# Fetching the next octet's gates and activations in quarters, spread over the weights of v, instead of whole

## The chip, the cores and the metric

The kernel runs on one core of a Trainium2 chip, in one launch. The metric is device time in microseconds (us). Three runs of the kernel before gave 2525.65, 2525.91 and 2526.83 us; their median, 2525.91, is the time before. A separate profiled execution took 2525.12 us. Engines: TensorE (PE), VectorE (DVE), ScalarE (ACT), GpSimd (POOL) and SyncE (SP), which here only issues DMAs.

## The reference, cut to what matters

The program is two transformer blocks on 512 tokens of width 1024. The first block and most of the second (attention, convolutions, gated mixing) lie ahead of the place of the change. The change lies in the last part, a layer with 16,384 experts of which every token uses 128:

```python
def chunk(args):
    hx, idx, g = args
    a = jax.nn.gelu(jnp.einsum("ced,cd->ce", u_emb[idx], hx), approximate=False)
    return jnp.einsum("ce,ced->cd", g * a, v_emb[idx])
...
x = x + peer(h2, w_peer_q[l], peer_sub_keys[l], peer_u[l], peer_v[l])
return rmsnorm_2(x, final_g)
```

For each token, 128 rows of the table `u_emb` are multiplied with the token, a gelu follows, and 128 rows of the table `v_emb` are summed with the weights `g * a`.

## The kernel before, in words

The 512 tokens are treated in two ways. For the last 384 tokens (`TD`) the kernel computes with all experts, as dense matrix products: the activations gelu(u·h) of all 16,384 experts, times a dense gate that is zero for unused experts, times v. For the first 128 tokens it gathers the used rows: 128 rows of u and then 128 rows of v per token. One gather brings one 128x1024 float32 tile (one row of the table per token, 512 KB) by an indirect DMA that POOL issues; DVE then consumes it with one instruction. There are 256 such row tiles in all (128 of u, 128 of v).

The dense part has two phases. In the u phase, 128 products of u are made in 16 groups of eight, called octets. Each octet's activations (a 128 x 8 x 384 tile, 1536 KB) go out to DRAM (`a_dr`), but for the last two octets, which stay (`NRES` = 2). The gates, made by one-hot products beside it, go to DRAM too (`g_dr`, 1536 KB per octet).

The v phase, in which the change lies, runs over 128 units (16 octets of 8) in the order `VORD`: the two octets that stayed, then the other 14. One unit is one 128x1024 slice of v (512 KB) and 24 matmuls of 384 columns on PE (`mix`, for 8 output tiles three products each of split high and low parts). For each unit:

- `weighted` (L1317) makes activation times gate on DVE (`wv`), its high part on ACT and its low part on DVE (`wv..l`). It runs `WAHEAD` = 2 units ahead of PE. It reads the gate tile `goct` (two buffers, one octet each) and the activation tile `acts` (two buffers, shown as `last` in the profile).
- `feed` (L255) loads v in pairs of units (1024 KB, tile `raw`, two buffers) on SP's DMA queue, and splits each unit: the high part on ACT (`w..h`), the low part on DVE (`w..l`). A pair is loaded as soon as both of its buffer's units are split. In unit `i` the program splits unit `i + 2`.
- `row_step` (L1054) consumes one or two gathered row tiles on DVE (`yt <- row, ea, yt` or `yt <- last, ea, yt`), so that all are done shortly before the end (`quota`). There are four row buffers (`NROW`): tiles named `row`, and the spare ends of the `last` tiles. POOL issues the gather into a buffer when DVE has consumed it.

Every engine works its instructions in the order in which the program was written, and so does each DMA queue: SP's queue carries the loads of v, of the gates and of the activations, in that order of issue; POOL's queue carries the gathers. What sets the order around the change is the main loop (L1355): at the first unit of an octet it issues `fetch_g` (the whole gate tile of the next octet) and `fetch_a` (its whole activation tile), both on SP's queue, then the rest of the unit. PE's `acc <- wv50l, w358h` is unit 50: the weights of unit n are named w(308+n), so unit 48, the first of octet 6, has wv48 and w356.

Of the kernel before, what the change touches and what calls it, by code (L numbers as in the profile page):

```python
# [10 lines left out]
F32 = mybir.dt.float32  # L11
# [10 lines left out]
P = 128  # L22
# [7 lines left out]
NOCT = 16  # L30
# [10 lines left out]
TC = 16  # L41
TD = T - P
NTC = TD // TC
WAHEAD = 2
NRES = 2
VORD = list(range(NOCT - 1, NOCT - 1 - NRES, -1)) + list(range(NOCT - NRES))
# [143 lines left out]
def body(tc, a):  # L190
    nc = tc.nc
# [4 lines left out]
    with ExitStack() as ctx:  # L196
        ctx.enter_context(tc.manual_schedule())

        def mkpool(stack, name, **k):
            return stack.enter_context(tc.tile_pool(name=name, bufs=1, **k))  # L200
# [90 lines left out]
        def unit(ahead=AHEAD):  # L291
            i = st["use"]
            feed(i + 1 + ahead)
            st["use"] += 1
            return parts.pop(i)
# [22 lines left out]
        wk = mkpool(ph, "wk")  # L318
# [440 lines left out]
        for g in range(2):  # L759
            c = 64 * g  # L760
# [248 lines left out]
        wk = mkpool(ph, "wk2")  # L1009
# [44 lines left out]
        def row_step():  # L1054


            n = rows[0]
            rows[0] += 1
            fetch_row(n + NROW)
            r, e = row_buf(n), ea[:, n % P:n % P + 1]  # L1060
            if n < P:
                V.tensor_tensor_reduce(r, r, h2t[0], 1.0, 0.0, ALU.mult, ALU.add, e)
            elif n == P:
                V.tensor_scalar(yts[0], r, e, None, ALU.mult)
            else:
                V.scalar_tensor_tensor(yts[0], r, e, yts[0], ALU.mult, ALU.add)
            if n == P - 1:
                S.activation(ea, ea, AF.Gelu)
                V.tensor_tensor(ea, ea, eg, ALU.mult)
# [114 lines left out]
        g_dr = dr.tile([NOCT, P, NTC, 8, TC], F32, name="g_dr")  # L1184
        a_dr = [dr.tile([P, 8, TD], F32, name=f"a_dr{o}") for o in range(NOCT - NRES)]
# [57 lines left out]
        aocts = {}  # L1243
        acts = []
# [42 lines left out]
        octs = {}  # L1287
        yts = []

        def last_phase():  # L1290

            nonlocal wk, ph, NT2
            ph.close()
            ph = ExitStack()
            ctx.enter_context(ph)
            wk = mkpool(ph, "wk3")
            NT2 = 12
            yts.append(wk.tile([P, D], F32, name="yt"))
            h2t.append(wk.tile([P, D], F32, name="h2s"))
            S.activation(h2t[1], h2tok, AF.Copy)  # L1300
            del h2t[0]
            fetch_g(0)

        def fetch_g(n):
            if n < NOCT:
                go = wk.tile([P, NTC, 8, TC], F32, tag="goct", name=f"goct{n}", bufs=2)
                nc.sync.dma_start(go, g_dr[VORD[n]])
                octs[n] = go

        def fetch_a(n):  # L1310
            if n < NOCT and VORD[n] not in aocts:
                aocts[VORD[n]] = acts[(n + 1) % 2]
                nc.sync.dma_start(aocts[VORD[n]], a_dr[VORD[n]])

        ready = {}

        def weighted(i):  # L1317

            n, j = divmod(i, 8)
            ao, go = aocts[VORD[n]], octs[n]  # L1320
            w, h, l = t2(f"wv{i}"), t2(f"wv{i}h", F32R), t2(f"wv{i}l", F32R)
            d = slice(P, T)
            V.tensor_tensor(w[:, d].rearrange("p (c t) -> p c t", c=NTC),
                            ao[:, j].rearrange("p (c t) -> p c t", c=NTC), go[:, :, j, :], ALU.mult)
            S.activation(h[:, d], w[:, d], AF.Copy)
            yield
            V.tensor_tensor(l[:, d], w[:, d], h[:, d].bitcast(F32), ALU.subtract)
            if i == 0:
                S.activation(l[:, :P], ident, AF.Copy, scale=0.0)
            if j == 7:  # L1330
                del octs[n]
            ready[i] = h, l
# [9 lines left out]
        def mix(m, q, first, last):  # L1342

            wh, wl, vh, vl = q
            c = slice(m * P, (m + 1) * P)
            d = slice(P, T)
            e = slice(0, T) if first else d
            PE.matmul(acc8[m][:, e], vh[:, c], wl[:, e], start=first, stop=False)
            PE.matmul(acc8[m][:, d], vl[:, c], wh[:, d], start=False, stop=False)
            PE.matmul(acc8[m][:, d], vh[:, c], wh[:, d], start=False, stop=last)  # L1350
# [2 lines left out]
        row0, yt = rows[0], yts[0]  # L1353
        NV = 8 * NOCT
        for i in range(NV - NLAST):  # L1355
            if i % 8 == 0:
                fetch_g(i // 8 + 1)
                fetch_a(i // 8 + 1)

            quota = min(2 * P, row0 + 4 + i * (2 * P - row0) // (NV - 12))  # L1360
            w = weighted(i + WAHEAD)
            next(w)
            if rows[0] < quota:
                row_step()
            list(w)
            while rows[0] < quota:
                row_step()
            q = ready.pop(i) + unit()
            for m in range(KT):
                mix(m, q, i == 0, False)  # L1370
# [152 lines left out]
```

## Time and profile before

| | before |
|---|---|
| median of 3 runs | 2525.91 us |
| profiled execution, its own time | 2525.12 us |
| its span, first to last instruction | 2523.4 us |
| PE busy over the span | 2404.9 us (95%) |
| DVE busy over the span | 1774.1 us (70%) |
| v phase, first product to the last octet's start | 1865.6 to 2470.5 us |

Times of the trace are counted from the first instruction. The v phase is the last quarter of the span. An octet's start is read off PE's timeline as the first product with that octet's first `wv`. In the views, "idle before" is the time for which an engine stood still ahead of an instruction, with what it waited for; "DMA share" is the mean busy share of 16 DMA engines (it can pass 1.00 by a little, as packets overlap at their ends), and "PEclk" is TensorE's granted clock as a share of its full speed. A matmul's shown duration includes its passage through the engine; the pace is read from start to start.

### The profile page before, as it was taken

To read this page: it belongs to the slowest core of one execution; us is meant where nothing else is said; L and a number is where in the kernel's file an instruction comes from. 1 tells how busy PE (TensorE), PEld (TensorE's weight loads), DVE (VectorE), ACT (ScalarE), POOL (GpSimd) and SP (SyncE) were. 2 spreads that over 40 slices of the span, in tenths; PEclk is the share of its full clock that TensorE was granted. 3 is DMA by queue.
4 is the path that set the end of the run, shared out by engine and by line. 5 is a ranking of instruction groups with operands and counts; after the bars stand their busy time and mean duration, and the time that the engine had idled before them with its cause. 6 is when DMAs were issued, how large, how long until landed. Compare 5 with 4: busy or idle time off the path is not lost.

```text
span 2523.4 us, 33808 instructions
## 1 busy us (share of the span) xinstructions
PE 2404.9 (95%) x13113; PEld 2135.8 (85%) x13121; DVE 1774.1 (70%) x3172; ACT 1022.2 (41%) x1558; POOL 747.6 (30%) x581
## 2 busy tenths in 40 slices
PE   9999999999999999999999999999998988898987
PEld 7777888888776668888899999999998988898887
DVE  4647644433468888556799999975577878787885
ACT  4454423322355665533233457653332323232333
POOL 2122011100137767003252300022234434444431
PEclk9999999999999999999999999999999999899998
DMA  4110222222211112222245568888889998999982
GB/s 164 57 51 34 105 100 85 99 101 100 84 51 51 51 51 100 85 99 92 91 155 189 184 219 266 270 303 300 305 305 373 331 368 334 371 337 361 358 322 90
DMA packets 128896, 466.13 MB, mean 185 GB/s; under 512 B 9184, under 2 KB 60512, under 8 KB 95200
## 3 DMA queue, kind: packets, MB, share of 16 engines
q1 hardware_dynamic: 39456, 281.04, 30.4%
q0 software_dynamic: 36864, 134.23, 14.7%
q10 hardware_dynamic: 52416, 48.70, 5.8%
q8 instruction: 103, 1.69, 0.3%
q14 instruction: 57, 0.47, 0.1%
HBM read 414.65 MB, written 49.28 MB: 184 GB/s over the span
## 4 chain that ended last, share of the span: by engine, by line
PE 44%; issue 25%; DVE 11%; DMA 10%; POOL 7%; ACT 3%; POOLq 0%; DVEq 0%; SPq 0%; ACTq 0%
PE u L133 8%; PE up L133 5%; DMA last<-in_vn,eid 5%; PE gate L133 5%; DMA row<-in_vn,eid 4%; PE pq L133 3%; POOL last L1045 3%; POOL row L1045 3%; PE acc L133 2%; PE wo L133 2%; DVE yt L133 2%; PE qkb L133 2%; PE ao L133 2%; PE gc L133 2%; PE co L133 2%
## 5 line engine op out<-in xcount | busy, mean ns | idle before, releaser
L133 POOL TENSOR_TENSOR cy<-cy,cvt 128x511 f32<-128x511 f32 (+14 forms) x120 | 170.7, 1422 | 59.2 <-ACT cvt L133 42.9
L1045 POOL DMA_INDIRECT last<-in_un,eid x64 | 74.0, 1156 | 342.2 <-DVE ea L133 317.4
L133 ACT ACTIVATE last<-u 128x384 f32<-128x384 f32 x128 | 63.4, 495 | 251.8 <-PE u L133 251.6
L1045 POOL DMA_INDIRECT last<-in_vn,eid x64 | 88.8, 1388 | 103.4 <-DVE yt L133 95.3
L1045 POOL DMA_INDIRECT row<-in_vn,eid x64 | 87.1, 1360 | 106.5 <-DVE yt L133 96.1
L1045 POOL DMA_INDIRECT row<-in_un,eid x64 | 75.7, 1183 | 123.4 <-DVE ea L133 120.7
L133 ACT ACTIVATE stage<-gp 128x512 f32<-128x512 f32 x96 | 95.9, 1106 | 36.7 <-PE gp L133 20.4
L133 DVE SCALAR_TENSOR_TENSOR yt<-row,ea,yt 128x1024 f32<-128x1024 f32 x64 | 82.1, 1283 | 37.1 <-DMA row<-in_vn,eid 37.1
L133 DVE SCALAR_TENSOR_TENSOR yt<-last,ea,yt 128x1024 f32<-128x1024 f32 x63 | 80.8, 1283 | 38.1 <-DMA last<-in_vn,eid 38.0
L133 DVE TENSOR_TENSOR hot<-hot,ijb 128x1024 bf16<-128x1024 bf16 x144 | 91.4, 687 | 1.6
L133 DVE SCALAR_TENSOR_TENSOR cyp<-u,par,cyp 128x511 f32<-128x511 f32 (+28 forms) x116 | 85.4, 736 | 2.4
L133 ACT ACTIVATE cvt<-u,par 128x511 f32<-128x511 f32 (+14 forms) x120 | 78.6, 701 | 0.7 <-DVE u L133 0.7
L133 PEld LDWEIGHTS <-hot 128*128 128x128 bf16 x1152 | 66.4, 97 | 13.1 <-DVE hot L133 8.5
L133 PE MATMUL gp<-hot,hot 128*128 128x128 bf16 x1152 | 74.7, 219 | 2.7 <-DVE hot L133 2.6
L133 DVE TENSOR_TENSOR wv<-last,goct 128x384 f32<-128x384 f32 x128 | 70.9, 554 | 0.0
L133 DVE TENSOR_TENSOR hot<-iota,ijb 128x1024 bf16<-128x1024 bf16 x96 | 61.8, 686 | 0.1
L133 DVE CUSTOM_DVE_ANT_0 last<-last,h2s 128x1024 f32<-128x1024 f32 x34 | 41.6, 1223 | 23.8 <-DMA last<-in_un,eid 23.8
L133 DVE CUSTOM_DVE_ANT_0 row<-row,h2s 128x1024 f32<-128x1024 f32 x36 | 44.0, 1223 | 12.5 <-DMA row<-in_un,eid 12.5
L133 DVE TENSOR_TENSOR su<-up,n2r 128x512 f32<-128x512 f32 x22 | 15.2, 691 | 51.7 <-PE up L133 51.7
L133 DVE MAX8 stop__8676<-skc 128x8 f32<-128x128 f32 x128 | 36.8, 287 | 5.5 <-ACT skc L133 3.2
L133 PEld LDWEIGHTS o<-v,pT 128*128 128x128 f32 x224 | 27.8, 191 | 14.8 <-ACT pT L133 7.6
L133 DVE CUSTOM_DVE_ANT_0 last<-last,h2tok 128x1024 f32<-128x1024 f32 x30 | 36.5, 1216 | 5.1 <-DMA last<-in_un,eid 5.1
(6461 smaller groups left out, 8606.2 us busy)
## 6 DMA issues: line engine op xcount, KB each, us to landing
raw<-in_w SPq DMA_DIRECT2D x89, 1024.0 KB, 4.8
raw<-in_u SPq DMA_DIRECT2D x64, 1024.0 KB, 6.4
raw<-in_v SPq DMA_DIRECT2D x64, 1024.0 KB, 7.7
g_dr<-stage ACTq DMA_DIRECT2D x24, 1024.0 KB, 7.0
goct<-g_dr SPq DMA_DIRECT2D x16, 1536.0 KB, 12.5
a_dr<-last ACTq DMA_DIRECT2D x14, 1536.0 KB, 10.0
last<-a_dr SPq DMA_DIRECT2D x14, 1536.0 KB, 17.3
xT<-in_x_t SPq DMA_DIRECT2D x1, 1024.0 KB, 9.5
```

Source lines behind the costliest of these rows:

```text
L133: return f(*args, **kw)
L1045: nc.gpsimd.indirect_dma_start(row_buf(n), None, t, bass.IndirectOffsetOnAxis(ap=eid[:, n % P:n % P + 1], axis=0))
```

## The change

The gate tile and the activation tile of the next octet are each fetched by four DMAs in place of one. The gates' quarters are cut by token (six of 24 groups of 16 tokens each), the activations' by product (two of eight). The gates' quarters are issued at units 0, 1, 2 and 3 of the running octet, the activations' at units 2, 3, 4 and 5. For octets that stayed (`n < NRES`) no activations are fetched, as before. The first gate tile is fetched in four DMAs as well, all at once.

```diff
-        def fetch_g(n):
-            if n < NOCT:
-                go = wk.tile([P, NTC, 8, TC], F32, tag="goct", name=f"goct{n}", bufs=2)
-                nc.sync.dma_start(go, g_dr[VORD[n]])
-                octs[n] = go
-
-        def fetch_a(n):
-            if n < NOCT and VORD[n] not in aocts:
-                aocts[VORD[n]] = acts[(n + 1) % 2]
-                nc.sync.dma_start(aocts[VORD[n]], a_dr[VORD[n]])
+        def fetch_g(n, quarters=range(4)):
+            for q in quarters if n < NOCT else ():
+                if q == 0:
+                    octs[n] = wk.tile([P, NTC, 8, TC], F32, tag="goct", name=f"goct{n}", bufs=2)
+                c = slice(q * NTC // 4, (q + 1) * NTC // 4)
+                nc.sync.dma_start(octs[n][:, c], g_dr[VORD[n]][:, c])
+
+        def fetch_a(n, q):
+            o = VORD[min(n, NOCT - 1)]
+            if n < NOCT and (q > 0 or o not in aocts) and n >= NRES:
+                aocts[o] = acts[(n + 1) % 2]
+                nc.sync.dma_start(aocts[o][:, 2 * q:2 * q + 2], a_dr[o][:, 2 * q:2 * q + 2])
...
         for i in range(NV - NLAST):
-            if i % 8 == 0:
-                fetch_g(i // 8 + 1)
-                fetch_a(i // 8 + 1)
+
+            n, j = divmod(i, 8)
+            if j < 4:
+                fetch_g(n + 1, (j,))
+            if 2 <= j < 6:
+                fetch_a(n + 1, j - 2)
```

On SP's queue, from the fetch of octet 6 (`goct6` and the activations `last1`) to that of octet 7, the program before has this order (`raw352` holds the weights w352 and w353):

```order
L1307 DMA goct6_17704<-g_dr_8686 128x3072
L1313 DMA last1_9505<-a_dr4_8691 128x3072
L273 DMA raw352_17717<-in_v 128x2048
L273 DMA raw354_17793<-in_v 128x2048
L273 DMA raw356_17871<-in_v 128x2048
L273 DMA raw358_17947<-in_v 128x2048
L1307 DMA goct7_18015<-g_dr_8686 128x3072
```

The changed program has this order on SP's queue for the same octet:

```order
L1309 DMA goct6_17734<-g_dr_8686 128x768
L273 DMA raw352_17746<-in_v 128x2048
L1309 DMA goct6_17734<-g_dr_8686 128x768 x2
L1315 DMA last1_9505<-a_dr4_8691 128x768
L273 DMA raw354_17825<-in_v 128x2048
L1309 DMA goct6_17734<-g_dr_8686 128x768
L1315 DMA last1_9505<-a_dr4_8691 128x768 x2
L273 DMA raw356_17906<-in_v 128x2048
L1315 DMA last1_9505<-a_dr4_8691 128x768
L273 DMA raw358_17983<-in_v 128x2048
L1309 DMA goct7_18051<-g_dr_8686 128x768
```

Two transfers of 3072 floats per partition at one place became eight of 768, of which one, three, three and one stand between the four loads of v.

On DVE, at the place where the weighted activations of octet 7 begin (`wv56`), the program before has:

```order
L133 TENSOR_TENSOR wv55l_18212<-wv55_18210,wv55h_18211 128x384 [waits Activation_49]
L133 SCALAR_TENSOR_TENSOR yt_15992<-last0_9504,ea_8671,yt_15992 128x1024 [waits DMASW0_49,DVE_49]
L133 TENSOR_TENSOR w363l_18221<-raw362_18104,w363h_18220 128x1024 [waits Activation_49]
L133 TENSOR_TENSOR wv56_18248<-last0_9504,goct7_18015 128x384 [waits DMAHW7_49,DMAHW6_49]
L133 SCALAR_TENSOR_TENSOR yt_15992<-last1_9505,ea_8671,yt_15992 128x1024 [waits DMASW1_49,DVE_49]
```

The changed program has there:

```order
L133 TENSOR_TENSOR wv55l_18254<-wv55_18252,wv55h_18253 128x384 [waits Activation_49]
L133 SCALAR_TENSOR_TENSOR yt_15992<-last0_9504,ea_8671,yt_15992 128x1024 [waits DMASW0_49,DVE_49]
L133 TENSOR_TENSOR w363l_18263<-raw362_18142,w363h_18262 128x1024 [waits Activation_49]
L133 TENSOR_TENSOR wv56_18290<-last0_9504,goct7_18051 128x384 [waits DMAHW5_49,DMAHW4_49,DMAHW6_49,DMAHW2_49,DMAHW0_49]
L133 SCALAR_TENSOR_TENSOR yt_15992<-last1_9505,ea_8671,yt_15992 128x1024 [waits DMASW1_49,DVE_49]
```

DVE's order is the same; `wv56` waits for five landings (four gate quarters, one activation quarter) in place of two. PE, ACT and POOL keep their orders as well.

## Rows read from the trace of the kernel before

**Rows 1.** Windows: start, length, busy us (count) of PE, PEld, DVE, ACT, POOL; PEclk, DMA share, GB/s.
```profile
1865.60:1900.00 34.40, 34.15 (x193) 33.51 (x194) 31.33 (x52) 10.38 (x15) 19.41 (x14) 1.00 0.83 294
1900.00:2431.20 531.20, 466.85 (x2497) 457.32 (x2496) 427.83 (x543) 154.44 (x210) 236.27 (x176) 0.93 0.93 354
2105.90:2146.50 40.60, 35.46 (x194) 34.98 (x193) 33.30 (x39) 11.43 (x16) 19.69 (x14) 0.92 0.94 359
2431.20:2470.50 39.30, 35.09 (x194) 34.75 (x193) 27.65 (x34) 13.02 (x18) 4.16 (x3) 0.96 0.67 259
```
**Rows 2.** PE's timeline around unit 50: start, duration, matmul, idle before it.
```profile
2113.89 0.34 PE L133 MATMUL acc<-wv49h,w357l 128*128 128x384 f32 x1
2114.06 0.34 PE L133 MATMUL acc<-wv49h,w357h 128*128 128x384 f32 x1
...
2119.89 0.69 PE L133 MATMUL acc<-wv50h,w358l 128*128 128x384 f32 x1 [5.14 <-DVE w358l L133]
```
**Rows 3.** DVE's timeline at the same place.
```profile
2112.43 1.28 DVE L133 SCALAR_TENSOR_TENSOR yt<-row,ea,yt 128x1024 f32<-128x1024 f32 x1 [2.48 <-DMA row<-in_vn,eid]
...
2117.41 1.28 DVE L133 SCALAR_TENSOR_TENSOR yt<-last,ea,yt 128x1024 f32<-128x1024 f32 x1 [3.23 <-DMA last<-in_vn,eid]
2118.61 1.22 DVE L133 TENSOR_TENSOR w358l<-raw,w358h 128x1024 fp32r<-128x1024 f32 x1
```
**Rows 4.** Waits of DVE from 1900 to 2431.2: total us, times, longest.
```profile
DVE yt L133 <- DMA row<-in_vn,eid: 35.4, 20, 4.6
DVE yt L133 <- DMA last<-in_vn,eid: 33.2, 18, 4.0
DVE last L133 <- DMA last<-in_un,eid: 20.8, 10, 3.9
DVE row L133 <- DMA row<-in_un,eid: 12.5, 9, 3.3
```
**Rows 5.** What the splits of `raw` waited for, 1900 to 2431.2: us, times.
```profile
  DMA raw<-in_v: 0.7, 2
```
**Rows 6.** DMA queues from 2107 to 2115: packets, MB, share of 16 engines.
```profile
q1 hardware_dynamic: 225, 2.57, 75.6%
q0 software_dynamic: 221, 0.82, 25.3%
```
**Rows 7.** Windows of 8 and 3 us inside octet 6.
```profile
2107.00:2115.00 8.00, 7.75 (x44) 7.26 (x42) 4.71 (x6) 1.48 (x3) 4.12 (x3) 1.00 1.02 425
2120.00:2123.00 3.00, 3.00 (x10) 3.00 (x11) 1.94 (x3) 1.47 (x2) 0.72 (x2) 0.50 1.03 412
2123.00:2126.00 3.00, 3.00 (x17) 3.00 (x16) 3.00 (x5) 1.24 (x2) 0.93 (x1) 0.88 0.53 154
```
**Rows 8.** DMA from 1900 to 2431.2: totals, POOL's queue, issues with median us to landing.
```profile
DMA packets 36548, 187.88 MB, mean 354 GB/s; under 512 B 4064, under 2 KB 4064, under 8 KB 26534
...
q0 software_dynamic: 25286, 92.05, 47.5%
...
raw<-in_v SPq DMA_DIRECT2D x52, 1024.0 KB, 8.1
...
last<-in_vn,eid POOLq DMA_INDIRECT x63, 7.4
row<-in_vn,eid POOLq DMA_INDIRECT x62, 8.2
```
**Rows 9.** Chain of waits from 2080 to 2130: start, us, what.
```profile
2090.26 8.98 DMA row<-in_vn,eid
...
2106.96 14.31 DMA last<-in_vn,eid
```
**Rows 10.** SP's timeline: start, duration of the issue.
```profile
2102.16 0.66 SPq L1307 DMA_DIRECT2D goct<-g_dr  x1
```
**Rows 11.** DMA issues of the whole run: count, KB each, median us to landing.
```profile
raw<-in_w SPq DMA_DIRECT2D x89, 1024.0 KB, 4.8
...
skeys<-in_sk SPq DMA_DIRECT2D x8, 128.0 KB, 2.4
```

## The prediction

> **What bounds the kernel now.** I read the windows by octet first, then the waits of DVE and PE's and DVE's timelines at the longest stall, and last the DMA queues in that stall. In octets 1 to 13 (1900.0 to 2431.2 us) an octet takes 531.2 / 13 = 40.86 us [rows 1]. PE's matmuls start 0.173 us apart when nothing holds them [rows 2], so the 2497 matmuls seen there need 432 us, or 33.3 us an octet. 99 us are lost, 7.6 an octet. 64.3 of them are PE's idle time (531.2 - 466.85). [...]
>
> The stall stands at the same place in nearly every octet, near its third unit. In octet 6 PE waits 5.14 us for w358l [rows 2]. DVE made that split late, and not because v was late: just ahead DVE stood 2.48 and 3.23 us for gathered rows [rows 3]. All splits of the 13 octets waited 0.7 us for loads of v [rows 5]; DVE waited 35.4 + 33.2 + 20.8 + 12.5 = 101.9 us for gathers [rows 4]. So the late thing is a row tile. The chain of waits shows one that needed 14.31 us to land [rows 9], where the median is 7.4 to 8.2 [rows 8].
>
> Why it is late is seen in the two DMA queues while gates and activations are fetched (2107 to 2115). SP's queue moved 225 packets and 2.57 MB, POOL's 221 packets and 0.82 MB [rows 6]: one packet each in turn, but SP's are of 12,288 bytes (3072 floats of a partition) and POOL's of 4096. The gathers got 0.82 / 8 = 103 GB/s. They need 92.05 MB / 13 = 7.08 MB an octet [rows 8], 13.5 tiles, which at PE's pace is 7.08 / 33.3 = 212 GB/s. In the some 10 us of the fetch two of four tiles are missing, and four row buffers cover no more. After it DVE runs without a pause to catch up (3.00 of 3.00 us) while the DMA share falls to 0.53 [rows 7]: the burst loses time twice.
>
> **The change, part by part.** *Packet size.* A quarter has 768 floats per partition, packets of 3072 bytes. With one packet each in turn the gathers get 4096 / 7168 = 57% beside it, of some 412 GB/s [rows 7] 235 GB/s, over the 212 they need. That is the main effect: the gathers no longer starve, wherever the quarters stand.
>
> *The same bytes.* The change moves no byte less: 187.88 MB / 13 = 14.45 MB an octet [rows 8]. At 412 GB/s, which 2120 to 2123 shows with gathers alone and which 2107 to 2115 passes (425) [rows 7], that is 35.1 us an octet. The same by shares: 3.15 MB of gates and activations at 177 GB/s take 17.8 us and let 4.18 MB of gathers pass; 4.19 MB of v at two thirds (8192-byte packets), 275 GB/s, take 15.2 us and let 2.09 MB pass; the last 0.81 MB of gathers take 2.0; the sum is 35.0. So DMA, not PE's 33.3, is the new floor.
>
> *More packets.* In 2107 to 2115 SP's queue used 75.6% of 16 x 8 us = 96.8 us, POOL's 32.4 [rows 6]; the difference, 64.4 us for 1.75 MB at nearly the same count, is 36.8 ns per KB, which leaves some 10 ns for a packet by itself. 768 packets more an octet on 16 engines: 768 x 0.010 / 16 = 0.5 us. Floor 35.6 us.
>
> *More transfers.* Eight in place of two an octet. SP spends 0.66 us on an issue [rows 10]; six more are 4 us of SP in 40, and SP issues nothing but these DMAs. What a transfer costs its queue beyond its bytes is not shown for 384 KB. From below: nothing, since the stretch with the end of the gates and the begin of the activations has a DMA share of 1.02 [rows 7]. From above: 128 KB land 2.4 us after issue and 1024 KB 4.8 [rows 11]; the line through both leaves 2.4 - 2.4 x 128 / 896 = 2.06 us at no bytes, and if the queue stood empty for it after each transfer, six more would cost 12.4 us of queue time. I take nothing, the nearer row, and keep the other end as a rival.
>
> *Order and waits.* Loads of v now stand behind one or three quarters. From one load to the next are two units, 8.3 to 9.3 us, in which three quarters and a load take 6.7 + 3.8 = 10.5 us; after two such intervals in a row a load starts up to 4.4 us late and lands, with 3.8 for itself and 2.06, 10.3 us after its issue. It is needed three units after it (12.5 us or more). Hidden, with 2 us to spare; beyond that ACT and DVE wait for v, with the gathers' consumption behind them. The new wait of wv56 for five landings: the last three quarters go out when w359 is split and wv56 comes five units later, 20.8 us, against 3.8 + 6.7 us of queue. Hidden; behind wv56 on DVE stand a row tile and the next split, so that a late quarter would stop PE a unit later.
>
> *The sum.* DMA can't be full all the time: row buffers wait for DVE, loads of v for splits. It was busy 0.93 on the mean [rows 1], with the dips in the catching up. I take 0.96 with the burst gone: 35.6 / 0.96 = 37.1 us an octet. Octets 1 to 13: 13 x (40.86 - 37.1) = 48.9 us. Octet 14 (39.3 us [rows 1]) has a burst but few gathers, 259 x 39.3 = 10.2 MB, so PE bounds it: 35.3 us, 4.0 saved. Octet 0 fetches gates only, and takes 34.4 us [rows 1]: 0. Octet 15 fetches nothing. Together 52.9. The profiled execution took 2525.1 us (span 2523.4 and 1.7 around it), 0.8 under the median: 2525.9 - 52.9 = 2473.
>
> **The rivals.** *A. As above*, 2473, own range 2455 to 2492 (octets of 35.7 to 38.6).
>
> *B. The wait for gathers is spread, not removed.* Four row buffers make a loop: 4 tiles pass in one landing and at least one consumption of 1.28 us [rows 3]. At PE's pace 4 tiles have 33.3 / 13.5 x 4 = 9.9 us, so landings must stay under 8.6 us. One before the burst, with only v beside it, took 8.98 [rows 9], and quarters are now beside most gathers. If all landings come to 10.2 us, 4 tiles take 11.5 and the octet 38.8: 2525.9 - 13 x 2.06 - 2 = 2497. For it: queues that are never empty. Against it: 57% of the bandwidth in place of 25% in the worst stretch.
>
> *C. There is no room.* If 354 GB/s, the mean of the 13 octets [rows 8], is what the memory gives, the octet stays at 40.8 and pays 0.5 for packets or wins as little: 2520 to 2531. Against it: 412 and 425 GB/s over 3 and 8 us [rows 7]. [...]
>
> *D. Slower: a fixed time per transfer that the queue waits out.* With 2.06 us of empty queue behind each of the twelve transfers of an octet, gathers fit into the gaps and the octet is 12 x 2.06 + 7.34 MB / 412 GB/s = 24.7 + 17.8 = 42.5 us: 2525.9 + 13 x 1.65 = 2547. It decides from (40.86 - 17.8) / 12 = 1.92 us a transfer. For it: the landings of small transfers [rows 11]. Against it: the share of 1.02 across a boundary of two transfers [rows 7]. [...]
>
> *E. The floor is reached*: octets at 35.6 and octet 14 at 33.3 give 2525.9 - 68.4 - 6 = 2451.
>
> **How the numbers follow.** A 0.58, B 0.20 (2492 to 2512), C 0.08, D 0.08, E 0.06. Within 0.2% (5 us) is what a measurement of this kernel can't tell from no change. Faster: A, B, E and half of C, 0.88; same: half of C, 0.04; slower: D, 0.08. The range 2452 to 2512 holds A, B and the edge of E, some 8 in 10.
>
> **What would show it.** Right: octets of 36 to 38.5 us; no stall of 4 us and more at the third unit; mean PEclk over 0.95; 375 to 395 GB/s over octets 1 to 13; in stretches with quarters, POOL's queue moving more bytes than SP's; DVE's waits for gathers under 55 us; landings of gathers below 9 us, loads of v at 9 to 10 without ACT or DVE waiting for them. B would show gathers landing over 10 us evenly, C the same 354 GB/s at a share near 1.00, D gaps in SP's queue between quarters. ACT or DVE waiting for `raw`, or wv56 and its like for `goct`, would refute my hidden waits; a stall that stays at the third unit would refute the packet turns as its cause.

## The result, and the profile after

The changed kernel takes 2466.99 us (median of four runs, 2463.47 to 2470.95) against 2526.37 us before in the runs beside it: a ratio of 0.9764, 95% interval [0.9747, 0.9781]. The forecast was 2473 us, 2452 to 2512. The span of the profiled execution went from 2523.4 to 2466.5 us, 56.9 us less.

The changed kernel's page, its span and the 40 slices of the granted clock, the DMA engines and their GB/s:

```profile
span 2466.5 us, 33918 instructions
...
PEclk9999999999999999999999999999999999999999
DMA  4111222222211112222244558779888999999992
GB/s 168 58 52 35 90 103 99 89 103 87 94 58 52 52 52 86 88 101 92 76 149 157 194 179 278 244 245 355 299 299 324 393 404 375 390 388 386 398 377 89
```

The granted clock is 0.9 or more in every slice, and the eight slices before the last one, which lie in the v phase, move 375 to 404 GB/s.

Windows of the changed kernel by octet (octet 0, octets 1 to 13, octet 6, octet 14), with the columns of [rows 1]:

```profile
1865.20:1899.00 33.80, 33.79 (x192) 33.47 (x193) 30.86 (x51) 10.33 (x14) 17.57 (x14) 1.00 0.90 329
1899.00:2380.10 481.10, 449.24 (x2498) 437.02 (x2497) 429.75 (x544) 154.40 (x209) 231.10 (x176) 0.99 1.00 390
2083.80:2120.40 36.60, 33.90 (x194) 33.15 (x193) 32.62 (x37) 11.44 (x16) 18.36 (x14) 1.00 0.99 387
2380.10:2413.90 33.80, 33.61 (x195) 33.28 (x194) 28.25 (x35) 13.40 (x19) 4.16 (x3) 1.00 0.80 307
```

Octets 1 to 13 take 481.1 / 13 = 37.01 us, where they took 40.86 [rows 1]: 50.1 us. Octet 14 gives 5.5 and octet 0 0.6. PE's idle time in octets 1 to 13 is 31.9 us (481.1 - 449.24) in place of 64.3, and the granted clock 0.99 in place of 0.93.

PE's timeline of the changed kernel at the place of the long stall [rows 2], and DVE's [rows 3]:

```profile
2092.13 0.34 PE L133 MATMUL acc<-wv50l,w358h 128*128 128x384 f32 x1
2092.30 0.40 PE L133 MATMUL acc<-wv50h,w358l 128*128 128x384 f32 x1
```

```profile
2088.11 1.29 DVE L133 SCALAR_TENSOR_TENSOR yt<-row,ea,yt 128x1024 f32<-128x1024 f32 x1 [0.25 <-DMA row<-in_vn,eid]
...
2090.98 1.22 DVE L133 TENSOR_TENSOR w358l<-raw,w358h 128x1024 fp32r<-128x1024 f32 x1
```

The 5.14 us before unit 50's second product are gone, because DVE waited 0.25 us for gathers ahead of w358l and not 2.48 and 3.23. PE's longest wait in octets 1 to 13 is now this (what waited, for what: us, times, longest):

```profile
PE acc L133 <- DVE w403l L133: 2.1, 1, 2.1
```

DVE's waits for gathers in octets 1 to 13 of the changed kernel, where [rows 4] had 101.9 us:

```profile
DVE yt L133 <- DMA row<-in_vn,eid: 17.9, 25, 1.5
DVE yt L133 <- DMA last<-in_vn,eid: 14.7, 21, 1.6
DVE row L133 <- DMA row<-in_un,eid: 10.2, 11, 1.9
DVE last L133 <- DMA last<-in_un,eid: 5.0, 7, 1.6
```

They are 47.8 us, in more and shorter pieces. What ACT's splits of v waited for in the same stretch (where [rows 5] had 0.7):

```profile
  DMA raw<-in_v: 5.0, 5
```

DMA queues of the changed kernel from 2093 to 2098, where three quarters are in flight (columns of [rows 6]), and the totals of octets 1 to 13:

```profile
q0 software_dynamic: 305, 1.12, 56.7%
q1 hardware_dynamic: 314, 0.87, 45.9%
...
DMA packets 47787, 187.81 MB, mean 390 GB/s; under 512 B 5310, under 2 KB 5310, under 8 KB 41129
```

POOL's queue moves 1.12 of 1.99 MB, 56%, beside quarters; beside whole tiles it moved 0.82 of 3.39 MB, 24% [rows 6]. The bytes are those of [rows 8]; the rate is 390 GB/s in place of 354.

The chain of waits of the changed kernel, the three gathers that stand in it around octet 6:

```profile
2078.79 9.23 DMA row<-in_vn,eid
...
2094.13 11.28 DMA last<-in_vn,eid
...
2114.79 10.14 DMA last<-in_vn,eid
```

Gathers are still links of the chain, but of 9 to 11 us, not 14 [rows 9].

### The profile page after: what moved, and what is told of

The parts are those of the page before. It is cut to its first block, busy times and chain, and to the rows that moved or that the text cites. A ratio compares the mean times of both kernels' runs of the same rounds, so it can differ in the third digit from the quotient of the medians.

```text
span 2466.5 us, 33918 instructions
## 1 busy us (share of the span) xinstructions
PE 2383.2 (97%) x13113; PEld 2111.7 (86%) x13121; DVE 1776.5 (72%) x3172; ACT 1021.6 (41%) x1558; POOL 740.2 (30%) x581
## 3 DMA queue, kind: packets, MB, share of 16 engines
q0 software_dynamic: 36864, 134.23, 14.3%
## 4 chain that ended last, share of the span: by engine, by line
PE 45%; issue 24%; DVE 10%; DMA 9%; POOL 7%; ACT 3%; POOLq 0%; DVEq 0%; SPq 0%; ACTq 0%
PE u L133 8%; DMA last<-in_vn,eid 6%; PE up L133 5%; PE gate L133 5%; DMA row<-in_vn,eid 3%; PE pq L133 3%; POOL row L1045 3%; POOL last L1045 3%; PE acc L133 2%; DVE yt L133 2%; PE wo L133 2%; PE qkb L133 2%; PE ao L133 2%; PE gc L133 2%; PE co L133 2%
```

## The experiments

The octet, the waits, the DMA share and the GB/s are of octets 1 to 13 of each kernel. Waits are sums over the groups of the view of waits; an octet is the stretch divided by 13. Each ratio is to runs of the kernel before that were made beside that kernel; their medians were 2526.4 to 2528.8 us.

| kernel | us an octet | DVE waits for gathers | ACT waits for v | DMA share, GB/s | time, us | ratio to before, interval |
|---|---|---|---|---|---|---|
| before | 40.86 | 101.9 | 0.7 | 0.93, 354 | 2526.4 | |
| changed | 37.01 | 47.8 | 5.0 | 1.00, 390 | 2467.0 | 0.9764 [0.9747, 0.9781] |
| quarters at one place | 43.70 | 28.8 | 127.9 | 0.87, 332 | 2566.2 | 1.0147 [1.0118, 1.0176] |
| spread, 32 neighbouring partitions | 49.08 | 200.4 | 3.1 | 0.97, 295 | 2643.4 | 1.0459 [1.0432, 1.0486] |
| spread, every fourth partition | 38.54 | 67.2 | 0 | 0.97, 376 | 2494.3 | 0.9863 [0.9846, 0.9879] |
| no activation fetch | 35.55 | 31.7 | 1.6 | 0.96, 363 | 2456.5 | 0.9721 [0.9705, 0.9737] |
| gathers to the end | 35.29 | 37.9 | 23.7 | 1.01, 397 | 2449.5 | 0.9693 [0.9674, 0.9711] |
| six row buffers | 35.07 | 0 | 49.4 | 1.02, 408 | 2451.7 | 0.9696 [0.9679, 0.9712] |
| POOL splits a quarter | 38.25 | 64.6 | 3.7 | 0.98, 378 | 2491.8 | 0.9859 [0.9842, 0.9875] |
| v in 4096-byte packets | 36.40 | 24.9 | 41.3 | 1.01, 397 | 2473.2 | 0.9784 [0.9765, 0.9802] |
| buffers and end together | 34.84 | 0 | 63.2 | 1.01, 399 | 2442.9 | 0.9670 [0.9651, 0.9689] |
| before, six row buffers | 37.08 | 42.4 | 53.6 | 0.99, 388 | 2473.7 | 0.9792 [0.9770, 0.9813] |

### Quarters at one place

```diff
-            if j < 4:
-                fetch_g(n + 1, (j,))
-            if 2 <= j < 6:
-                fetch_a(n + 1, j - 2)
+            if j == 0:
+                fetch_g(n + 1)
+                for q in range(4):
+                    fetch_a(n + 1, q)
```

> All eight quarters (packets of 3072 bytes) are issued at the first unit of the octet, none between the loads of v. Theory P (packets take turns one for one, so large packets on SP's queue starve the gathers): the gathers keep 57% of the bandwidth beside the burst and don't starve, so DVE's waits for gathers stay near the 48 us of the changed kernel in octets 1 to 13; the price is that the burst fills SP's queue for 17.8 us and the next load of v stands behind it, 1 to 3 us late once an octet: octets of 37.5 to 39 us, 2474 to 2493 us in all, with ACT and DVE now waiting for raw. Theory S (the burst itself, its place and length, is what costs, not the packet size): no gain over the kernel before, 2505 to 2526 us, with DVE's waits for gathers near 100 us as before.

It is slower than the kernel before: 2566 us. DMA from 2166 to 2176, in one burst of quarters (the two queues, then the load of v and the gathers issued in that stretch, with their us to landing):

```profile
q0 software_dynamic: 601, 2.16, 53.8%
q1 hardware_dynamic: 697, 1.91, 48.8%
...
raw<-in_v SPq DMA_DIRECT2D x1, 1024.0 KB, 18.8
...
row<-in_vn,eid POOLq DMA_INDIRECT x2, 9.7
last<-in_vn,eid POOLq DMA_INDIRECT x2, 9.0
```

The gathers issued in the burst of the kernel before (2107 to 2115, the stretch of [rows 6]) took longer to land:

```profile
row<-in_vn,eid POOLq DMA_INDIRECT x2, 12.2
last<-in_vn,eid POOLq DMA_INDIRECT x1, 14.3
```

DVE's timeline just after it, and ACT's longest waits for v in octets 1 to 13:

```profile
2181.87 1.28 DVE L133 SCALAR_TENSOR_TENSOR yt<-last,ea,yt 128x1024 f32<-128x1024 f32 x1 [2.50 <-DMA last<-in_vn,eid]
2189.15 1.23 DVE L133 TENSOR_TENSOR w368l<-raw,w368h 128x1024 fp32r<-128x1024 f32 x1 [6.00 <-ACT w368h L133]
```

```profile
ACT w336h L133 <- DMA raw<-in_v: 11.5, 1, 11.5
ACT w360h L133 <- DMA raw<-in_v: 11.0, 1, 11.0
```

Theory P is right about the gathers: they get 53% in the burst, land there in 9.0 to 9.7 us and not in 12.2 to 14.3, and DVE's waits for them are the lowest of all kernels with four row buffers and whole traffic but one. Part of that low sum may come of DVE standing for v, which gives the gathers time; the landings in the burst, before v is late, don't depend on it.

P is also right that v is late, but far too low on the price: the load of v behind the burst lands 18.8 us after its issue, and ACT waits 127.9 / 13 = 9.8 us an octet for v, not 1 to 3. What the gathers gain in the burst, SP's queue loses: it moves 1.91 MB in 10 us here and 2.57 MB in 8 us in the kernel before [rows 6], so that 3.15 MB of gates and activations take some 16.5 us in place of 9.8 (an estimate from these two stretches). Small packets without the new places cost 39 us; S, which expected no change, misses too.

### The same places, wide packets

```diff
-                c = slice(q * NTC // 4, (q + 1) * NTC // 4)
-                nc.sync.dma_start(octs[n][:, c], g_dr[VORD[n]][:, c])
+                c = slice(q * P // 4, (q + 1) * P // 4)
+                nc.sync.dma_start(octs[n][c], g_dr[VORD[n]][c])
```

The activations are cut in the same way. In the second of the two kernels `c` is `slice(q, P, 4)`.

> The quarters stay where the change put them but are cut by partition (32 partitions of 3072 floats, packets of 12,288 bytes) in place of by token or product. Theory P, taken strictly: beside each quarter the gathers get 25% again, for the same 9.8 us an octet in all, so most of the stall stays: octets of 39 to 40.5 us, 2492 to 2515 us, DVE's waits for gathers over 80 us. Theory S: pieces of 1.2 us are too short to run four row buffers dry, and the total of bytes decides: as the changed kernel, 2460 to 2475 us, octets of 36.5 to 37.5 us, DVE's waits for gathers near 48 us.

> The quarters again in packets of 12,288 bytes and at the changed kernel's places, but each takes every fourth partition (q, q+4, ...) in place of 32 neighbouring ones. In the kernel with neighbouring partitions SP's queue took 50% of 16 x 638 us for 12,483 packets, where the kernel before took 45.5% of 16 x 531 us for 11,230: its wide packets took about twice as long each. Theory N (transfers into few neighbouring partitions are slow in themselves): with every fourth partition the packets are as short as before, and the place and packet size alone decide: 2460 to 2475 us if pieces of 1.2 us can't run four row buffers dry (S), 2492 to 2515 us if 25% beside each piece starves the gathers as before (P). Without N (small partition counts are slow however they lie): 2600 us and more again, GB/s near 295.

With neighbouring partitions it took 2643 us, beyond both theories. A window of that kernel with one quarter after another in flight (2212 to 2215), and SP's queue in its octets 1 to 13:

```profile
2212.00:2215.00 3.00, 3.00 (x19) 3.00 (x19) 1.45 (x2) 1.29 (x2) 1.15 (x2) 1.00 0.90 168
```

```profile
q1 hardware_dynamic: 12483, 95.45, 50.0%
```

The engines count as busy (0.90) and move 168 GB/s. The next run took the same packets over every fourth partition; its octets 1 to 13, the two longest groups of DVE's waits, and SP's queue:

```profile
1902.40:2403.40 501.00, 455.69 (x2498) 443.43 (x2498) 430.14 (x545) 154.11 (x210) 233.01 (x176) 0.97 0.97 376
```

```profile
DVE yt L133 <- DMA last<-in_vn,eid: 23.8, 17, 2.7
DVE yt L133 <- DMA row<-in_vn,eid: 22.9, 21, 2.4
```

```profile
q1 hardware_dynamic: 12508, 95.64, 49.1%
```

A packet of SP's queue takes 0.491 x 16 x 501 / 12508 = 315 ns on the mean, against 409 with neighbouring partitions: theory N holds, and the first of the two runs says nothing on P and S. The second does: 2494 us is just inside P's range and above S's, while its octets (38.54 us) and its waits for gathers (67.2 us) lie between what the two theories gave for the first run. New places alone, with wide packets, bring octets from 40.86 to 38.54 us, 2.3 of the change's 3.85; the small packets, added to them, bring the other 1.5 and cut the waits for gathers from 67.2 to 47.8 us. The split holds in this order only: added first, the small packets made the octet 2.8 us longer (43.70).

### No activation fetch

```diff
-                nc.sync.dma_start(aocts[o][:, 2 * q:2 * q + 2], a_dr[o][:, 2 * q:2 * q + 2])
```

> Leaves out the eight-product activation fetch of octets 2 to 15 (56 transfers of 384 KB; the products are made with activations that are not theirs), everything else as the changed kernel. Theory F (the bytes are the floor of the changed kernel): 14.45 - 1.57 = 12.88 MB an octet at 390 to 412 GB/s are 31.3 to 33.0 us, under PE's 33.3, so octets 2 to 13 fall from 37.0 to 33.5 to 34.5 us and the time to 2425 to 2438 us, DMA share near 0.93. Theory L (the loop of four row buffers with landings of 9 us is the floor): the gathers and the loads of v are the same, landings fall by less than 1 us, octets stay above 36 us, 2452 to 2462 us.

```profile
1902.90:2365.10 462.20, 441.50 (x2499) 432.81 (x2498) 428.66 (x545) 154.73 (x210) 237.81 (x176) 1.00 0.96 363
```

F misses. L's time holds (2456.5 us), and its octets miss by little: 35.55 us and not above 36, at 363 GB/s, when 408 can be had (next run). The 1.57 MB that are gone from an octet are 3.8 us at 408 GB/s, and 1.5 came. DVE still waits 31.7 us for gathers, and DVE's own 428.7 us and those waits make 460.4 of the 462.2 us. So bytes alone were not what held the changed kernel at 37.0.

### Six row buffers

```diff
+            bufs_.extend(wk.tile([P, D], F32, name=f"spare{i}") for i in range(2))
+            nrow[0] += 2
             fetch_g(0)
...
-            fetch_row(n + NROW)
+            fetch_row(n + nrow[0])
...
+            bufs_.append(held.pop(n))
```

A gather takes the buffer that has been free for longest (`held[n] = bufs_.pop(0)`).

> The changed kernel with two more row buffers from the start of the v phase (six in place of four). In octets 1 to 13 DVE's own work (429.8 us) and its waits for gathers (47.8) make up 477.6 of 481.1 us. Theory V (DVE is the engine that never rests, and an octet is its 33.0 us plus its waits for gathers, which come of four buffers against landings of some 9 us): the waits fall to 10 to 25 us, octets to 34.0 to 35.5, the time to 2437 to 2450 us. Theory F (the bytes: DMA share is 1.00 already): more gathers in flight only lengthen each landing and push v later; octets stay at 36.3 to 37, 2457 to 2468 us, with ACT's waits for raw growing from 5 us to 20 and more.

Octets 1 to 13, and ACT's longest wait for v:

```profile
1902.30:2358.20 455.90, 442.47 (x2497) 431.18 (x2495) 419.91 (x537) 155.04 (x207) 235.70 (x174) 1.00 1.02 408
```

```profile
ACT w324h L133 <- DMA raw<-in_v: 3.9, 1, 3.9
```

DVE waits for no gather any more, where V kept 10 to 25 us. 35.07 us an octet lies in V's forecast; the time, 2451.7 us, lies 2 us above V's range. 408 GB/s at a share of 1.02 is the byte floor that F spoke of, reached here and not before, and the waits turn to v (49.4 us), as F said. The octets also carry a little less here, some 186 MB (408 GB/s over 455.9 us) for 187.8; all the bytes at this rate would be 35.4 us an octet. The changed kernel stood 1.6 us an octet over that floor, for want of row buffers.

### Before, with six row buffers

The same edit in the kernel before, whose fetches stay whole and at one place.

> The kernel before (gates and activations whole, at the first unit of the octet) with two more row buffers in the v phase, nothing else. The prediction said that in the burst two of four tiles are missing and four row buffers cover no more. If the starved gathers are the whole of the stall, two more buffers cover the two tiles: DVE's waits for gathers fall from 102 us to 20 to 40 in octets 1 to 13, octets to 36.5 to 38, 2465 to 2490 us. If wide packets harm beyond the missing tiles (loads of v then come late behind the burst, as in the kernel with all quarters at one place), octets stay at 39 to 41 us, 2500 to 2530 us, and ACT waits for raw.

Its octets 1 to 13, and the two longest groups of DVE's waits:

```profile
1899.90:2381.90 482.00, 453.99 (x2498) 444.18 (x2497) 423.76 (x539) 154.81 (x209) 235.27 (x174) 0.97 0.99 388
```

```profile
DVE yt L133 <- DMA spare<-in_vn,eid: 12.9, 7, 2.8
DVE yt L133 <- DMA last<-in_vn,eid: 12.7, 8, 2.3
```

2474 us, 37.08 an octet: two buffers alone take nearly as much from the kernel before as the change does (2.1% and 2.4% of the time, 49.2 and 50.1 us in octets 1 to 13). That shows what its stall was: too few row tiles at hand while the gates and activations are fetched. That exactly two were missing is not shown, as DVE still waits 42.4 us for gathers, a little over the 20 to 40 expected. The second theory is right in one part: with the gathers less late, v is late, and ACT waits 53.6 us for it.

### POOL splits a quarter, and v in packets of 4096 bytes

```diff
+            if i >= NU_BASE + 128:
+                return G if i % 4 == 3 else V
```

> The changed kernel with the low split of every fourth unit of v (1.2 us on DVE) on POOL, where it took 2.4 us in the u phase. Theory V: DVE's own work falls by 2.3 us an octet; if POOL's gathers are not held up the time falls by 13 x 2.3 = 30 us to about 2437; POOL issues its next gather up to 2.4 us later twice an octet, so the waits for gathers may give a third back: 2435 to 2450 us. Theory F: the freed time turns into waits for gathers, 2458 to 2468 us. The rival against both, that POOL's delay of the gathers costs more than DVE gains: over 2470 us.

Slower than the changed kernel: 2492 us. DVE's groups of that kernel in octets 1 to 13 (count, busy us, mean ns of one):

```profile
L133 DVE SCALAR_TENSOR_TENSOR yt<-row,ea,yt 128x1024 f32<-128x1024 f32 x60 | 88.4, 1473 | 21.5 <-DMA row<-in_vn,eid 21.3
L133 DVE SCALAR_TENSOR_TENSOR yt<-last,ea,yt 128x1024 f32<-128x1024 f32 x60 | 83.7, 1395 | 28.3 <-DMA last<-in_vn,eid 28.3
```

DVE lost 27 instructions and no time (431.06 us of busy, 429.75 in the changed kernel): what took 1.28 us [rows 3] takes 1.4 to 1.5 on the mean. The mean hides what happens to a single one. POOL's split of unit 87, and DVE's `yt` beside it:

```profile
2273.04 3.10 POOL L133 TENSOR_TENSOR w395l<-raw,w395h 128x1024 fp32r<-128x1024 f32 x1
```

```profile
2273.86 3.36 DVE L133 SCALAR_TENSOR_TENSOR yt<-row,ea,yt 128x1024 f32<-128x1024 f32 x1
```

This `yt` ends 1.1 us after POOL's split does. Away from POOL's splits a `yt` of this trace took 1.27 us (at 2098.89 us), and in the changed kernel, which has none of them in these octets, the mean is 1.28. The waits for gathers rose to 64.6 us as well, as the rival said, and PE now waits 13.0 us for POOL's splits. That DVE would gain nothing, no theory said.

```diff
-                    raws[j // 2] = wp.tile([P, 2, D], F32, tag="raw", name=f"raw{j}", bufs=2)
+                    raws[j // 2] = wp.tile([P, 2, D + 8], F32, tag="raw", name=f"raw{j}", bufs=2)[:, :, :D]
```

> The changed kernel with 32 bytes of room between the two units of a raw tile, so that a load of v goes in packets of 4096 bytes in place of 8192 (same bytes, one transfer). Theory P: with one packet in turn the gathers get half of the bandwidth beside v, not a third; DVE's waits for gathers fall from 47.8 to 25 to 40 us in octets 1 to 13, loads of v take 1 to 2 us longer and stay hidden: 2448 to 2462 us. If the waits for gathers don't come of the stretches with v, or the longer loads come late: 2463 to 2475 us.

Octets fell to 36.40 us, the waits for gathers to 24.9, but ACT's waits for v rose to 41.3: the longer loads did come late, as the second case said. The time, 2473 us, is in that case's range and can't be told from the changed kernel's (the intervals overlap). In its profiled execution octet 1 began 6 us later than in the changed kernel's; the same tile holds the weights of all phases, and whether that is its price was not tried.

### The gathers to the end, and a better version

```diff
-            quota = min(2 * P, row0 + 4 + i * (2 * P - row0) // (NV - 12))
+            quota = min(2 * P, row0 + 4 + i * (2 * P - row0) // (NV - 5))
```

> The gathers are spread over 123 units in place of 116 (quota divides by NV - 5, not NV - 12), the rest as the changed kernel. Theory F: 194 tiles over 123 units are 12.6 an octet in place of 13.5, 14.0 MB in place of 14.45, so octets 1 to 13 go from 37.0 to about 35.9 us (-14 us); octets 14 and 15 take some 11 tiles more, where the DMA share was 0.80 and lower, at a price of 0 to 4 us: 2452 to 2460 us. The rival, that the end is what decides (the last gathers are consumed just ahead of the last products and DVE's sum over them ends late): no gain or a loss, 2465 to 2480 us.

```profile
1899.90:2358.70 458.80, 439.90 (x2499) 431.33 (x2497) 415.59 (x532) 154.56 (x208) 213.88 (x166) 1.00 1.01 397
```

2449.5 us, a little under the range. Fewer gathers an octet are fewer bytes (182.1 MB for 187.8) and less work for DVE (415.6 us for 429.8); octets 14 and 15 had room: the stretch behind octet 13 takes 88.0 us, where it took 86.4. The last gathers don't hold the end.

> The changed kernel with six row buffers and with the gathers spread over 123 units, both together. With six buffers the DMA engines moved 408 GB/s at a share of 1.02 and DVE no longer waited for gathers, so bytes are what is left: 182 MB / 13 = 14.0 MB an octet at 408 GB/s are 34.3 us in place of 35.07, 13 x 0.75 = 10 us under the six buffers' 2452: 2438 to 2446 us, octets 1 to 13 near 34.3 us, DMA share 1.00 to 1.02 still. If the bytes were not the floor, the two gains (15 and 17 us under the changed kernel) would add up: 2432 to 2437 us, octets at PE's 33.3. If the late gathers hold up the end: 2447 us and more.

```profile
1900.80:2353.70 452.90, 441.12 (x2497) 433.25 (x2496) 408.19 (x528) 155.47 (x207) 210.24 (x165) 1.00 1.01 399
```

2442.9 us, the lowest median of all, 3.3% under the kernel before and 1% under the change. As the byte floor says, the gains of the two don't add up: 34.84 us an octet, with ACT waiting 63.2 us for v. The rate is 399 GB/s and not the 408 of the sum, so the octet is half a us over its 34.3. The interval overlaps those of its two parts a little; that it is faster than either is likely, not shown.

## Why the prediction was right

The cause of the stall, the gathers' share from packets in turn and the floor were right. What it called the main effect was too strong, and the last term of its sum, 0.96, was right by luck.

- **The cause.** Gathers starved by the burst, not v: shown. Two more row buffers in the kernel before, with nothing else changed, cut the waits for gathers from 101.9 to 42.4 us and the time by nearly as much as the change.
- **Packets in turn.** 57% for the gathers beside quarters was forecast, 56% is measured in the changed kernel, 53% in the burst of quarters. The packets of POOL's queue and of SP's were 305 and 314 in the one stretch, 601 and 697 in the other: near equal counts, which is what the views show of the turns. In the burst of quarters gathers land in 9.0 to 9.7 us and not in 12.2 to 14.3.
- **"That is the main effect: the gathers no longer starve, wherever the quarters stand".** The sentence's end holds, its weight does not. With the quarters at one place the gathers don't starve and the kernel is 1.5% slower than before. The new places give 2.3 of 3.85 us an octet by themselves, the packets, on top of them, 1.5.
- **Order and waits.** Hidden, as forecast: 5.0 us of waits for v in 13 octets, and no wait for `goct` among DVE's. How much margin was left is not shown; with all eight quarters ahead of it, a load of v came late by 9.8 us an octet on the mean.
- **More transfers.** Rival D is out. The octet is 37.0 us, not 42.5, and in the burst of eight quarters both queues together fill the engines (48.8% and 53.8%): 1.91 MB, some 4.9 quarters, passed in 10 us, 2.1 us for each with whatever gap there was, where a gap alone would have been 2.06. The kernel moves 390 GB/s in octets 1 to 13 with 384 KB transfers and 354 with the 1536 KB ones. The rate of one such transfer by itself is not shown.
- **No room (C).** Out: 390 GB/s over 481 us in the changed kernel, 408 over 456 us with six buffers.
- **The floor and 0.96.** The floor of 35.0 to 35.6 us was right: 35.07 with six buffers, 35.4 if they carried all the bytes. The term 0.96 came out right by luck of its parts: the share was not 0.96 of engines at 412 GB/s but 1.00 at 390. And what held the octet at 37.0 was not the engines' idling but rival B's loop of four buffers, in a mild form. By that loop an octet of 37.0 us goes with landings of 37.0 x 4 / 13.5 - 1.28 = 9.7 us (an estimate), and the gathers in the chain took 9.23, 11.28 and 10.14. So one of the prediction's signs did not come: landings below 9 us. The prediction left out the account that fits the kernels with four buffers in which v isn't late: an octet is DVE's own work and its waits for gathers. Before: 427.8 + 101.9 = 529.7 of 531.2 us; changed: 429.8 + 47.8 = 477.6 of 481.1.
- **The edges.** Octet 14 came to 33.8 us, not 35.3, and octet 0 fell by 0.6: with octets 1 to 13 at 50.1 for 48.9 us, these make up 3.3 of the 4 us between 52.9 and 56.9.

## What to carry to other kernels

When several DMA queues feed one engine in order, look at how many bytes each packet of the rival queue carries and how many tiles the buffers cover during its longest transfer; a stall that names a late gather may be the price of a big load beside it (here the gathers moved 24% of the bytes beside whole tiles and 56% beside quarters). Smaller packets and spread places were worth having together: small packets alone handed the wait to what stood behind them in their own queue, the loads of v, for which ACT waited 127.9 us in octets 1 to 13, and 5.0 with the new places. Then add up the busiest in-order engine's own work and its waits: where that is the span, try buffers for what it waits for: two of 512 KB were worth nearly as much here as cutting and moving the loads (37.08 and 37.01 us an octet), and both together came down to the bytes' floor (35.07 us at 408 GB/s).

## What the runs showed of the hardware

- Transfers into 32 neighbouring partitions were slow: 168 GB/s in a stretch of 3 us with mostly such packets, 295 GB/s over octets 1 to 13, where the same packets to every fourth partition left 376; a packet of SP's queue took 409 ns on the mean, against 315. The reason is not shown.
- Beside a 128x1024 split on POOL a `yt` of DVE took longer: 3.36 us in the lines shown, against 1.27 away from one. Over all `yt` of octets 1 to 13 the means were 1.40 and 1.47 us, against 1.28 in the changed kernel, whose splits are DVE's. The reason is not shown.
- The DMA engines' mean share said little of the rate: over octets 1 to 13, 0.97 went with 295 GB/s and with 376, 1.02 with 408.
